# A decoder step on one core: lent token places that hold raw weights longer

## The chip, the cores and the metric

The kernel is one program on one core of a Trainium2 chip. The time is the device time of one execution in microseconds (us); lower is better. Engines are named as the profile names them: PE is TensorE (PEld its weight loads), DVE is VectorE, ACT is ScalarE, POOL is GpSimd, SP is SyncE, whose queue issues most loads. SBUF is the on-chip memory, PSUM holds TensorE's sums.

## What is computed

One step of a hybrid decoder layer, on 2048 prompt tokens and 64 new tokens (8 sequences of 8) that attend to 8192 cached positions through a page table. All data are float32.

```
h  = rmsnorm(x, g1);  z = h @ w_in                     # 1024 -> 3072: B, C, U, Q, K, V
y_conv = B * conv3(C * U)                              # 512 channels, width 3
o  = softmax(q1 k1 + alibi) v - lam * softmax(q2 k2 + alibi) v   # 4 heads, causal
o  = rmsnorm(o, subln) * (1 - lam0)
x  = x + concat(y_conv, o) @ w_out                     # 1024 -> 1024
h2 = rmsnorm(x, g2)
x  = x + relu(h2 @ w_up)**2 @ w_down                   # 1024 -> 4096 -> 1024
y  = rmsnorm(x, final_g)
```

The outputs are y for prompt and new tokens, the keys, the values and the last two rows of C * U.

## The kernel before

**Products in three parts.** A float32 product is made of three: each operand is split into a high half in a reduced format and the rest as a low half, and TensorE adds high x high, high x low and low x high. A raw weight (`wraw`, 128 x 1024, 512 KB) is loaded through SP's queue, ScalarE makes its high half `wh` (L254), VectorE its low half `wl` (L256), and TensorE reads those two. There are four buffers for each of `wh` and `wl`, and two places of its own for raw weights.

**Stages.** First the input projection, then the prompt's attention, together with the last convolution and the first tokens' output projection. From about 1140 us on it is output projection and MLP: four blocks of 384 prompt tokens (blocks 0 to 3, three tiles of 128 rows) and then a last block with 512 prompt tokens and the 64 new ones. Beside blocks 0 to 3 runs decoding: attention of the new tokens to the cached pages. It is a generator whose small steps are emitted between TensorE's matmuls (`between`, `tick`), a fixed amount for so much matmul time. It gathers keys and values on GpSimd's queue (`kraw`, `vpg`, L727 and L735), transposes the keys on VectorE (`kt`, L745), and does small matmuls (L930, L965, L977).

**A block** (`Dense.run`). The MLP's 4096 columns are 32 units m in 16 chunks c of two units. `first_ups` makes four up units; then for c = 0 to 13 `down` takes the two units of chunk c (36 matmuls, x += ..., L1445), and `up` makes the two of chunk c + 2 (48 matmuls). The last two up units (c = 13) are made together in two halves, after each of which `before_last(g)` is called: it issues the loads of the next tokens' mixed activations (`load_mix`, four loads of 0.8 MB). Then come the down chunk 14, the output projection of the *next* block's tokens (`out_proj`), and the down chunk 15. Between chunks `poll` takes one entry of a list `rest`: the final norms and stores of the block before, loads of gains, and lending.

**The order of the weights** is written out by `mlp_weights`: u0 to u3; for c = 0 to 13 the two of down chunk c and the two of up chunk c + 2; down 14; eight of the output projection (four pairs of rows for each half of the 1024 columns); down 15: 72 in a block. `W.get()` takes the next, `W.ahead(n)` has the n after it split. When weight i is split, `back` frees its place and loads the raw weights as far as i + 2 (two places), or i + 5 while three places are lent. `out_proj` makes the first half of the columns for all three token tiles, weight by weight (72 matmuls), and adds to x after that (L1340); then the second half tile by tile (72 matmuls).

**Lending.** Token tiles lie in six places: `x1_0` and `x1_1`, three each, for even and odd blocks. Between the storing of one block's results and the loading of the block after the next, three are empty. `W.lend` makes them extra places for raw weights: in block 0 after c = 0, in blocks 1 to 3 at the twelfth entry of `rest`, that is at the end of c = 3. Before the change `take_back` ends this after c = 9: from then on the lent places are not refilled. After c = 11 `x_loads` puts the loads of the next tokens (`load_x`, L1274, 512 KB each) on `rest`, one for each poll. In block 3 the tokens of the last block are loaded in `before_last(0)`.

Emission is by hand (`manual_schedule`): each engine and queue takes its instructions in the order in which the program issues them, and waits for data and places by semaphores.

Of the kernel before, what the change touches and what calls it, by code (L numbers as in the profile page):

```python
# [62 lines left out]
NDS = 4  # L63
# [4 lines left out]
def tile_hymba_step(  # L68
# [124 lines left out]
    def drain():  # L193
        while dec["gen"] is not None:
            step()
# [8 lines left out]
    class Weights:  # L204
# [9 lines left out]
        def lend(self, slots):  # L214

            self.lent = list(slots)
            self.extra += slots
            self.load(len(self.srcs))

        def take_back(self):  # L220

            self.lent, self.extra = [], []

        def back(self, i):

            slot = self.held.pop(i, None)
            if slot is None:
                self.own += 1
            elif slot in self.lent:
                self.extra.append(slot)  # L230
            self.load(i + 1 + self.rb + len(self.lent))

        lent = []
# [107 lines left out]
    W = Weights(lo, [wview[:, :, c0:c0 + P] for o in orders for _, _, c0 in o], 2, 2)  # L341
# [797 lines left out]
    for j in range(1, 4 * H):  # L1139
        h, g = divmod(j, 4)  # L1140
        after = gidx[16 * ((j - 5) // 4) + 15] if j >= 5 else -1
        due.setdefault(max(gidx[4 * j] - 3, after, -1), []).append((load_k, h, g))
        after = gidx[16 * ((j - VB) // 4) + 15] + 3 if j >= VB else -1
        due.setdefault(max(gidx[4 * j], after), []).append((load_v, h, g))
    for j in range(1, 8 * H):
        after = gidx[2 * (j - 3) + 1] if j >= 3 else -1
# [41 lines left out]
    NC = NF // CH  # L1188
# [27 lines left out]
    class Dense:  # L1216
# [261 lines left out]
                                               op0=ALU.mult, op1=ALU.mult)  # L1478
                eng.dma_start(out=dst[r0:r0 + n, :], in_=y[:n])

        def run(self, ub, poll, before_last, nxt, after, x_loads=lambda: None):
            self.ub = ub
            self.first_ups()
            for c in range(NC - 2):
                self.down(range(c * CH, (c + 1) * CH))
                poll()
                if c == NC - 7:
                    W.take_back()
                if c == NC - 5:
                    x_loads()  # L1490
                ms = range((c + 2) * CH, (c + 3) * CH)
                if c < NC - 3:
                    for m in ms:
                        self.up(m)
                        poll()
# [598 lines left out]
    sb1 = c1.enter_context(tc.tile_pool(name="mlp_sb1", bufs=1, reuse_waits="tile"))  # L2094
# [3 lines left out]
    box = {}  # L2098
    rest = []
# [2 lines left out]

        rest.append(lambda: W.lend([(xb, f"x1_{(i + 1) % 2}{ti}") for ti in range(3)]))

    def x_loads():
        while rest:
            rest.pop(0)()
        assert not W.held
        nxt = ds[cur[0] + 1] if cur[0] < NDS - 1 else None
        if nxt:  # L2110
            rest.extend(lambda ti=ti: nxt.load_x(ti) for ti in range(3))

    lend(0)

# [15 lines left out]
    def poll():  # L2130
        switch()
        if rest:
            rest.pop(0)()
        elif box and box["todo"] and cur[0] == NDS - 1:
            box["todo"].pop(0)()

    def before_last(g):
        while rest:
            rest.pop(0)()
        if cur[0] < NDS - 1:  # L2140
            ds[cur[0] + 1].load_mix(0, [g])
            return
        drain()
        switch()
        while box["todo"]:
            box["todo"].pop(0)()
        if g == 0:
            for ti in range(3):
                box["d"].load_x(ti)

    cur = [0]
    for i, d in enumerate(ds):
        cur[0] = i
        d.run([(sb1, "uh", "ul", 4, 384)], poll, before_last, lambda: ds[cur[0] + 1] if cur[0] < NDS - 1 else box["d"], None, x_loads)
        rest += [lambda: load_gain("f", nc.gpsimd)] + FN * [lambda: None]
        for ti in range(4):
            rest += [lambda d=d, ti=ti: d.final(ti, nc.gpsimd), lambda: None]
        if i < NDS - 1:
            rest.append(lambda: load_gain("2", nc.gpsimd))
        if i < NDS - 1:  # L2160
            lend(i + 1)
# [40 lines left out]
```

## Time and profile before

| | us |
|---|---|
| three runs, median (lowest to highest) | 3179.14 (3163.96 to 3181.11) |
| the profiled execution, its own time | 3178.61 |
| its span from first to last instruction | 3176.7 |
| TensorE busy in it | 3024.5 |
| mean granted TensorE clock (1 is 2.4 GHz) | 0.982 |

The profile is of one execution. A line such as L254 is a line of the kernel; "out<-in" gives the tiles by the program's names. Busy time counts overlapping instructions once; what ended an idle time stands behind an arrow. A clock below 1.00 in a stretch means that TensorE was granted its lower level (1.2 GHz) for a part of it. The DMA share is the mean busy share of the core's 16 DMA engines. A matmul's own record is longer than its pace, since matmuls overlap.

### The profile page before, as it was taken

Reading aid. Unit: us, or ns where it says so; the run is one execution under the profiler, and the core shown is the slowest. Engines: PE = TensorE matmul, PEld = TensorE weight load, DVE = VectorE, ACT = ScalarE, POOL = GpSimd, SP = SyncE. Lnnn points to the kernel's source line nnn. Section 1 sums busy time; section 2 is a strip of 40 time slices with the busy share of each in tenths; the row PEclk is TensorE's granted clock in tenths of the full one; section 3 lists DMA queues with packets and bytes.
Section 4 is the critical chain, followed back from the end, with each engine's and each line's share of the span. In section 5 each row is a group of like instructions: output and inputs, shape, how many; then the busy total and the mean of one; then the engine's idle time right before and its main releaser. Section 6 shows DMA issues by size and latency. Waiting matters only on the chain.

```text
span 3176.7 us, 55329 instructions
## 1 busy us (share of the span) xinstructions
PE 3024.5 (95%) x21670; PEld 2590.5 (82%) x21670; DVE 1956.6 (62%) x4121; ACT 1334.2 (42%) x2873; POOL 779.9 (25%) x1002
## 2 busy tenths in 40 slices
PE   7998998999999999998999999999999999999998
PEld 7987888989997788876778767787677887888887
DVE  5466353277888667766676666776566554664445
ACT  3323323367778643342334324433334433333332
POOL 1012364311122120122434443444324430000000
PEclk9999999999999999999999999999999999999999
DMA  5766886744435356676788786887767756232222
GB/s 153 226 226 202 292 283 196 248 126 106 124 102 153 110 183 209 210 249 231 246 275 285 247 293 229 287 290 264 273 204 248 248 164 201 73 100 80 80 80 70
DMA packets 443294, 624.73 MB, mean 197 GB/s; under 512 B 36661, under 2 KB 337717, under 8 KB 426650
## 3 DMA queue, kind: packets, MB, share of 16 engines
q1 hardware_dynamic: 379594, 338.82, 34.4%
q0 software_dynamic: 62272, 278.96, 24.9%
q8 instruction: 171, 2.80, 0.4%
q10 hardware_dynamic: 1168, 3.41, 0.3%
q14 instruction: 89, 0.73, 0.1%
HBM read 565.35 MB, written 55.74 MB: 196 GB/s over the span
## 4 chain that ended last, share of the span: by engine, by line
PE 70%; DVE 10%; DMA 9%; issue 5%; ACT 3%; POOL 3%; SPq 0%; ACTq 0%; DVEq 0%; POOLq 0%
PE ups L200 7%; PE dps L1438 6%; PE ups L202 6%; PE ups L201 6%; PE dps L1439 6%; PE dps L1440 6%; PE ps L200 5%; PE ps L202 5%; PE ps L201 5%; PE asc L1864 4%; DMA wraw<-in_w_up_dram 3%; PE O L1951 3%; PE sps L930 3%; PE o_ps L977 3%; DVE kt L745 2%
## 5 line engine op out<-in xcount | busy, mean ns | idle before, releaser
L256 DVE TENSOR_TENSOR wl<-wraw,wh 128x1024 fp32r<-128x1024 f32 x408 | 497.7, 1220 | 330.4 <-ACT wh L254 324.7
L254 ACT CAST wh<-wraw 128x1024 fp32r<-128x1024 f32 x408 | 424.3, 1048 | 598.2 <-PE dps L1440 257.9
L735 POOL DMA_INDIRECT vpg<-in_cache_v_dram,pt x512 | 533.6, 1042 | 323.8 <-PE o_ps L977 178.6
L200 PE MATMUL ups<-h2h,wh 128*128 128x384 f32 (+2 forms) x1520 | 506.5, 333 | 14.2 <-DVE x L1445 8.1
L202 PE MATMUL ups<-h2h,wl 128*128 128x384 f32 (+2 forms) x1520 | 493.2, 324 | 3.9 <-DVE wl L256 3.9
L201 PE MATMUL ups<-h2l,wh 128*128 128x384 f32 (+2 forms) x1520 | 492.1, 324 | 0.0
L1438 PE MATMUL dps<-wh,uh 128*128 128x512 f32 (+1 forms) x1076 | 436.9, 406 | 7.3 <-ACT wh L254 4.7
L1439 PE MATMUL dps<-wl,uh 128*128 128x512 f32 (+1 forms) x1076 | 426.7, 397 | 14.9 <-DVE wl L256 14.2
L1445 DVE TENSOR_TENSOR x<-dps,x 128x512 f32<-128x512 f32 (+1 forms) x534 | 356.2, 681 | 114.8 <-PE dps L1440 114.1
L1440 PE MATMUL dps<-wh,ul 128*128 128x512 f32 (+1 forms) x1076 | 424.4, 394 | 0.0
L200 PE MATMUL ps<-hh,wh 128*128 128x384 f32 (+1 forms) x1152 | 404.9, 351 | 1.1 <-ACT cc L1558 0.7
L202 PE MATMUL ps<-hh,wl 128*128 128x384 f32 (+1 forms) x1152 | 377.7, 328 | 2.9 <-DVE wl L256 2.9
L201 PE MATMUL ps<-hl,wh 128*128 128x384 f32 (+1 forms) x1152 | 376.7, 327 | 0.1
L727 POOL DMA_INDIRECT kraw<-in_cache_k_dram,idxk x128 | 125.6, 982 | 938.9 <-DVE kt L745 922.4
L200 PEld LDWEIGHTS ups<-h2h,wh 128*128 128x128 f32 x1520 | 288.1, 190 | 49.2 <-issue 35.5
L1397 DVE TENSOR_TENSOR ul<-r,uh 128x384 fp32r<-128x384 f32 (+2 forms) x190 | 99.9, 526 | 370.4 <-ACT uh L1396 370.2
L745 DVE STREAM_TRANSPOSE kt<-kraw 128x512 f32<-128x512 f32 x512 | 317.7, 678 | 0.0
L202 PEld LDWEIGHTS ups<-h2h,wl 128*128 128x128 f32 x1520 | 288.0, 189 | 4.8 <-DVE wl L256 4.8
L201 PEld LDWEIGHTS ups<-h2l,wh 128*128 128x128 f32 x1520 | 288.4, 190 | 2.3
L1394 ACT ACTIVATE r<-ups 128x384 f32<-128x384 f32 (+2 forms) x190 | 88.2, 464 | 423.1 <-PE ups L202 423.1
L1438 PEld LDWEIGHTS dps<-wh,uh 128*128 128x128 f32 (+1 forms) x1076 | 200.2, 186 | 75.6 <-issue 23.8
L1439 PEld LDWEIGHTS dps<-wl,uh 128*128 128x128 f32 (+1 forms) x1076 | 200.6, 186 | 61.2 <-DVE wl L256 23.0
(273 smaller groups left out, 4764.3 us busy)
## 6 DMA issues: line engine op xcount, KB each, us to landing
wraw<-in_w_up_dram SPq DMA_DIRECT2D x160, 512.0 KB
wraw<-in_w_down_dram SPq DMA_DIRECT2D x160, 512.0 KB
wraw<-in_w_in_dram SPq DMA_DIRECT2D x72, 512.0 KB
wraw<-in_w_out_dram SPq DMA_DIRECT2D x40, 512.0 KB
x<-in_x_prompt_dram SPq DMA_DIRECT2D x27, 512.0 KB
vpg<-in_cache_v_dram,pt POOLq DMA_INDIRECT x512
qt<-QH SPq DMA_DIRECT2D x64, 128.0 KB
qt<-QL SPq DMA_DIRECT2D x64, 128.0 KB
```

The lines of the kernel that those rows point to most:

```text
L200: nc.tensor.matmul(ps, lhsT=wh, rhs=ah, start=first, stop=False)
L201: nc.tensor.matmul(ps, lhsT=wh, rhs=al, start=False, stop=False)
L202: nc.tensor.matmul(ps, lhsT=wl, rhs=ah, start=False, stop=last)
L254: nc.scalar.copy(wh, t)
L256: eng.tensor_sub(wl, t, wh.bitcast(F32))
L735: nc.gpsimd.indirect_dma_start(out=t[:, g, :], out_offset=None, in_=cv, in_offset=bass.IndirectOffsetOnAxis(ap=idxv[:, 4 * it + g:4 * it + ...
L745: nc.vector.transpose(t[:, e, 16 * j:16 * j + 16].rearrange("p a b -> p (a b)"), kraw[2 * r + e][:, 16 * j:16 * j + 16].rearrange("p a b - ...
L1438: nc.tensor.matmul(ps, lhsT=uh, rhs=wh[:, half], start=(i == 0), stop=False)
L1439: nc.tensor.matmul(ps, lhsT=uh, rhs=wl[:, half], start=False, stop=False)
L1440: nc.tensor.matmul(ps, lhsT=ul, rhs=wh[:, half], start=False, stop=(i == len(ms) - 1))
L1445: nc.vector.tensor_add(xx, ps, xx)
L1864: nc.tensor.matmul(ps[:, 0:N], lhsT=t[self.h, qg][:, c, qo:qo + P], rhs=kst[self.h, kc][:, c, 0:N], start=(k == 0), stop=(k == 1))
```

## The change

`take_back` moves from after c = 9 to `before_last`: behind the second half of the last up chunks in blocks 0 to 2, behind the first in block 3. It is given a function that loads a token tile into a place. Empty lent places get their tokens at once. A place that holds a raw weight gets them when that weight has been split: `back` then calls the function in place of returning the place. `x_loads` with its two calls in `run` is gone, and so are the three token loads of `before_last(0)` in block 3.

```diff
--- before.py
+++ after.py
@@ -217,9 +217,12 @@
             self.extra += slots
             self.load(len(self.srcs))
 
-        def take_back(self):
-
-            self.lent, self.extra = [], []
+        def take_back(self, freed):
+
+            self.freed = freed
+            empty, self.lent, self.extra = self.extra, [], []
+            for slot in empty:
+                freed(slot)
 
         def back(self, i):
 
@@ -228,6 +231,8 @@
                 self.own += 1
             elif slot in self.lent:
                 self.extra.append(slot)
+            else:
+                self.freed(slot)
             self.load(i + 1 + self.rb + len(self.lent))
 
         lent = []
@@ -1478,16 +1483,12 @@
                                                op0=ALU.mult, op1=ALU.mult)
                 eng.dma_start(out=dst[r0:r0 + n, :], in_=y[:n])
 
-        def run(self, ub, poll, before_last, nxt, after, x_loads=lambda: None):
+        def run(self, ub, poll, before_last, nxt, after):
             self.ub = ub
             self.first_ups()
             for c in range(NC - 2):
                 self.down(range(c * CH, (c + 1) * CH))
                 poll()
-                if c == NC - 7:
-                    W.take_back()
-                if c == NC - 5:
-                    x_loads()
                 ms = range((c + 2) * CH, (c + 3) * CH)
                 if c < NC - 3:
                     for m in ms:
@@ -2102,13 +2103,8 @@
 
         rest.append(lambda: W.lend([(xb, f"x1_{(i + 1) % 2}{ti}") for ti in range(3)]))
 
-    def x_loads():
-        while rest:
-            rest.pop(0)()
-        assert not W.held
-        nxt = ds[cur[0] + 1] if cur[0] < NDS - 1 else None
-        if nxt:
-            rest.extend(lambda ti=ti: nxt.load_x(ti) for ti in range(3))
+    def take_back(d):
+        W.take_back(lambda slot: d.load_x([t for _, t in d.xslots].index(slot[1])))
 
     lend(0)
 
@@ -2139,19 +2135,20 @@
             rest.pop(0)()
         if cur[0] < NDS - 1:
             ds[cur[0] + 1].load_mix(0, [g])
+            if g == 1:
+                take_back(ds[cur[0] + 1])
             return
         drain()
         switch()
         while box["todo"]:
             box["todo"].pop(0)()
         if g == 0:
-            for ti in range(3):
-                box["d"].load_x(ti)
+            take_back(box["d"])
 
     cur = [0]
     for i, d in enumerate(ds):
         cur[0] = i
-        d.run([(sb1, "uh", "ul", 4, 384)], poll, before_last, lambda: ds[cur[0] + 1] if cur[0] < NDS - 1 else box["d"], None, x_loads)
+        d.run([(sb1, "uh", "ul", 4, 384)], poll, before_last, lambda: ds[cur[0] + 1] if cur[0] < NDS - 1 else box["d"], None)
         rest += [lambda: load_gain("f", nc.gpsimd)] + FN * [lambda: None]
         for ti in range(4):
             rest += [lambda d=d, ti=ti: d.final(ti, nc.gpsimd), lambda: None]
```

## Rows read from the trace of the kernel before

**Rows 1.** The page's busy time by engine, and its group of ScalarE's high halves.

```profile
PE 3024.5 (95%) x21670; PEld 2590.5 (82%) x21670; DVE 1956.6 (62%) x4121; ACT 1334.2 (42%) x2873; POOL 779.9 (25%) x1002
...
L254 ACT CAST wh<-wraw 128x1024 fp32r<-128x1024 f32 x408 | 424.3, 1048 | 598.2 <-PE dps L1440 257.9
```

**Rows 2.** Waits of the whole span: who waited for whom, total, times, longest.

```profile
ACT wh L254 <- DMA wraw<-in_w_out_dram: 104.9, 27, 9.8
```

**Rows 3.** Windows: length, busy time by engine, clock, DMA share, GB/s.

```profile
2654.23:2662.44 8.21, 8.21 (x38) 6.71 (x37) 4.48 (x7) 2.48 (x4) 0.00 (x0) 1.00 1.03 328
1656.98:1678.82 21.84, 21.84 (x185) 17.70 (x184) 14.84 (x25) 8.61 (x17) 10.07 (x10) 1.00 0.82 289
1396.39:1422.12 25.73, 23.63 (x186) 18.90 (x185) 14.86 (x24) 8.80 (x16) 9.93 (x11) 0.93 0.86 274
1433.14:1457.11 23.97, 22.58 (x176) 15.86 (x174) 9.99 (x13) 6.78 (x11) 10.06 (x10) 1.00 0.96 348
1457.11:1483.53 26.42, 21.43 (x140) 16.25 (x137) 16.20 (x38) 7.00 (x10) 9.54 (x10) 0.87 0.64 227
1779.30:1803.56 24.26, 21.45 (x156) 17.97 (x155) 16.97 (x35) 8.06 (x13) 11.06 (x11) 0.93 0.73 249
1856.88:1884.50 27.62, 23.80 (x173) 17.19 (x172) 13.88 (x21) 6.75 (x11) 9.33 (x10) 0.94 0.80 273
1884.50:1907.82 23.32, 20.37 (x110) 14.35 (x109) 13.05 (x29) 7.04 (x14) 7.41 (x8) 1.00 0.66 234
2273.88:2295.54 21.66, 20.62 (x167) 14.72 (x166) 8.74 (x12) 5.92 (x11) 9.64 (x10) 1.00 1.00 374
2295.54:2325.12 29.58, 25.41 (x161) 17.87 (x160) 17.88 (x40) 7.92 (x11) 10.71 (x10) 0.88 0.59 217
2662.44:2723.64 61.20, 59.41 (x265) 44.38 (x264) 29.91 (x58) 16.15 (x22) 0.00 (x0) 1.00 0.20 69
```

**Rows 4.** Chain of waits behind block 0: start, length, what.

```profile
1419.95 15.26 DMA wraw<-in_w_out_dram
...
1437.62 7.42 DMA wraw<-in_w_out_dram
...
1447.45 7.07 DMA wraw<-in_w_out_dram
...
1462.38 1.77 DVE x L1340 x3
```

**Rows 5.** Chain of waits behind block 1.

```profile
1861.53 9.77 DMA wraw<-in_w_out_dram
...
1881.43 10.36 DMA wraw<-in_w_out_dram
```

**Rows 6.** VectorE's timeline at the projection behind block 2.

```profile
2294.25 1.23 DVE L256 TENSOR_TENSOR wl<-wraw,wh 128x1024 fp32r<-128x1024 f32 x1 [5.89 <-ACT wh L254]
...
2296.08 3.08 DVE L745 STREAM_TRANSPOSE kt<-kraw 128x512 f32<-128x512 f32 x5
...
2300.19 1.89 DVE L745 STREAM_TRANSPOSE kt<-kraw 128x512 f32<-128x512 f32 x3
2302.00 1.85 DVE L1340 TENSOR_TENSOR x<-ps,x 128x512 f32<-128x512 f32 x3
2303.77 1.21 DVE L256 TENSOR_TENSOR wl<-wraw,wh 128x1024 fp32r<-128x1024 f32 x1
```

**Rows 7.** VectorE's timeline in block 1, c = 11.

```profile
1783.49 1.23 DVE L256 TENSOR_TENSOR wl<-wraw,wh 128x1024 fp32r<-128x1024 f32 x1 [1.00 <-ACT wh L254]
```

**Rows 8.** SyncE's queue in block 0: the first and last of three token loads.

```profile
1365.36 0.98 SPq L1274 DMA_DIRECT2D x<-in_x_prompt_dram  x1
...
1387.77 0.43 SPq L1274 DMA_DIRECT2D x<-in_x_prompt_dram  x1
```

**Rows 9.** Chain of waits behind block 2 and in block 3.

```profile
2318.11 30.97 issue
...
2379.97 13.22 DMA wraw<-in_w_up_dram
```

## Prediction

> **What bounds the kernel now.** Begin with the engines: TensorE is busy 95% of the span [rows 1], so time can only be won where TensorE stands still or runs at its lower clock. The waits name the candidate for this change: ScalarE, which makes the high half of each weight (L254, 1.05 us [rows 1]), waited 27 times, 104.9 us in all, for the output projection's weights to land [rows 2]. That is ScalarE's idle time, not the kernel's. What of it reaches TensorE is read from stretches of equal work [rows 3]. Call T the start of a block's output projection (for the next tokens), 1433.14, 1856.88 and 2273.88 us for the projections behind blocks 0, 1 and 2. Number a block's weights as the list has them: 56 and 57 are the down weights of c = 13, 58 and 59 the last up weights, 60 and 61 the down weights of c = 14, 62 to 69 the projection's, 70 and 71 the last down weights.
>
> In the lent part of a block one pair of chunks takes 21.84 us with TensorE full and clock 1.00 (block 1, c = 5). The same work takes 25.73 us at c = 13 of block 0, and 24.26 at c = 11 of block 1, both behind the present take-back. The projection's first half takes 23.97, 27.62 and 21.66 us in the three blocks, its second half 26.42, 23.32 and 29.58, though a half is the same 72 matmuls with some decoding between. DMA is at 0.80 to 1.00 in the first halves and 0.59 to 0.66 in the second [rows 3].
>
> The chain of waits shows why. Behind block 0 it runs from one projection weight's landing to the next: 15.26, 7.42 and 7.07 us, then through VectorE's three additions at 1462.38 [rows 4]. Behind block 1 it is 9.77 and 10.36 us of the same [rows 5]. With two places, the load of weight i+2 cannot begin before weight i is split, so each landing sets the next. VectorE takes its instructions in order, and makes the trouble larger: behind block 2 the low half at 2294.25 waited 5.89 us, and behind it stood eight transposes for decoding (4.97 us), three additions (1.85) and then the low half that TensorE was waiting for, at 2303.77, 8 us after the second half had begun at 2295.54 [rows 3, 6].
>
> **The change part by part.** *What stays.* No matmul, split or byte is added. Three places take a token tile each and are loaded as often as before. So the sum is of waits alone.
>
> *Take-back at the last up chunks in place of c = 9.* After c = 9 the lead of raw weights no longer falls from five to two. Block 0, c = 13: 25.73 - 21.84 = 3.9 us gained. Block 1, c = 11: 2.4 us between the same two kinds of stretch, but VectorE idled only 1.00 us for the weight's high half [rows 7], and what follows there is decoding's step from one sequence to the next; I take 1.0, with bounds 0 and 2.4. The stall that I see in block 2's c = 11 and 12 belongs to that step too: 0.
>
> *The first half of the projection.* At the new take-back weights 62 to 66 lie raw in the five places. Of the eight, five are on chip before T, where now 64 is loading. I take block 2's first half as that of unhurried weights: it has the same decoding (167 TensorE instructions against 176 and 173) and clock 1.00. Gain 23.97 - 21.66 = 2.3 and 27.62 - 21.66 = 6.0, together 8.3 us.
>
> *The second half.* Its bare length: 36 matmuls take 8.21 us where nothing interferes [rows 3], so 72 take 16.4. Block 2's first half is 5.3 us above that for 95 instructions of decoding, 0.055 each. The second halves have 68, 38 and 89 more than 72, so they should take 20.2, 18.5 and 21.3 us; they are 6.2, 4.8 and 8.3 above it, 19.3 together, the low clock (0.87, 1.00, 0.88) included. Not all of it goes. Weights 68 and 69 need buffers that come free late, and their low halves are queued on VectorE behind the three additions: 1.85 + 2 x 1.23 us, against the 12 matmuls (2.7 us) that TensorE can do with 66 and 67: 1.5 us stays. Weight 69 goes out when 67 is split, about T + 18, and TensorE wants it 18 matmuls (4.1 us) into the second half, at T + 26; with the landings of 7 to 10 us above and 2.3 us of splitting it is 1 to 4 us late, on top of nothing that the 1.5 covers: another 1.5, the nearer end, since DMA is down to about 0.6 by then. With 3 us left in each of three blocks the gain is 19.3 - 9 = 10.3; bounds 0 (the gap stays) and 14.8 (only the first 1.5 stays).
>
> *The token loads, moved.* Now they go out early, in block 0 the first at 1365.36 and the last of the three at 1387.77, 75 us before the additions want them [rows 4, 8]. After the change each goes out on SP right behind the split of a lent weight. In which order follows from the lending, and when from the half's four quarters of 5.4 us (21.66 / 4): 64 is split at its start, 65, 66 and 67 with the second, third and fourth quarter, each split taking 1.05 + 1.23 us. In blocks 1 and 2 the two own places hold 22 and 23 when three more are lent, and places are refilled in turn, so 62 and 63 are own and 64, 65, 66 lent: tokens go out at about T + 2, T + 5 and T + 11. In block 0 lending comes at weights 8 and 9, so lent are 62, 65 and 66: about T - 9 (ahead of c = 14's down chunk, half of a 21.84 us pair), T + 5 and T + 11. They are wanted when the first half ends, T + 21.7 or later. From T + 11 there are 10.7 us; two of the three landings in rows 4 and both in rows 5 fit. On SP nothing but weights stands behind a token's load, and the one directly behind (67 or 68) waits for the same split or an earlier one, so SP adds no wait. But an own place stays empty from the split of 63 to that of 65, since loading then stops two weights ahead: the lead of five is spent once, in the projection, and not renewed. If a token is late, the addition blocks VectorE, and the low halves of 68 and 69 and then TensorE wait behind it. I take 1 us in each of three blocks, 3 in all; bounds 0 and 4.6 each (a landing of 15.26, as in rows 4).
>
> The Trainium skill speaks against this move: "DMA: Bandwidth & Descriptors", under Rules for kernel authors, says to issue a DMA early and wait for it late, so that its fixed cost is covered. By that rule the token loads should stay where they are; what it would cost here is the third rival below. The rows show the same rule broken today for the weights, whose landings are the chain.
>
> *Block 3.* Decoding has ended and DMA is at 0.20 in the projection behind it, from 2662.44 on [rows 3]; I count 0. The last block never lends.
>
> The sum: 3.9 + 1.0 + 8.3 + 10.3 - 3 = 20.5 us. The profiled execution took 3178.61 us (span 3176.7 and 1.9 outside it), the median of the three runs is 3179.14, so it stands for them. 3178.6 - 20.5 = 3158; with the small stalls that I have not named shifting a little either way, 3159. By its own bounds the likeliest case lies between 3178.6 - (3.9 + 2.4 + 8.3 + 14.8) = 3149 (no token late, only 1.5 us left in each second half) and 3163 (5.4 us won in the second halves in place of 10.3).
>
> A difference of 0.5% (16 us) is about what a measurement of this kernel can tell from none: its three runs span 17 us.
>
> **The rivals.** *The gap of the second half stays.* The same 1.5 MB that were tokens early are now in the projection, where DMA is at 1.00 and 374 GB/s in block 2's first half [rows 3]: 4 us of that bandwidth. If 67 to 69 are late by as much as they now are, only 3.9 + 1.0 + 8.3 - 3 = 10 us are won: 3168. For it: the DMA share. Against it: total bytes from take-back to the end of the projection are equal, three tokens for three weights, and tokens are wanted last.
>
> *Decoding and the short lead of the next block take it back.* Behind block 2 the chain runs over GpSimd's gathers, with a 30.97 us stretch that shows no reason, and then over a landing of 13.22 us in block 3's first chunks, where there are only two places before and after the change [rows 9]. If gathers and those landings set the pace, what is saved behind block 2 (8.3 - 3 - 1 = 4 us) and behind block 1 (6.0 + 4.8 - 3 - 1 = 7 us) is waited for again: a gain of 20.5 - 11 = 9 us, 3169. Against it: the row names no cause, and by the code a gather of keys is issued when VectorE has transposed the keys before it, which comes earlier too.
>
> *Tokens late: slower.* The three last landings before an addition decide. From a landing of 10.7 us on, each further us is a us of TensorE in each of three blocks. The gains above must be used up first: at 10.7 + 20/3 = 17.4 us the time is as before, at 23 us it is 3195. The longest landing in these rows is 15.26 us, in the midst of 3 MB of loads for the activations. That is what the rule of the Trainium skill named above would make of the change.
>
> *The change does not do what it says* (the lead is already lost before T, as when SP is held up by the activations' loads, which stay in front): 3176 to 3179.
>
> **How the numbers follow.** Chances: forecast 0.55, second half unchanged 0.22, taken back 0.13, tokens late 0.06, no effect 0.04. The time given is the forecast's. Eight in ten: from 3144 (the forecast's lower bound and the spread of runs) to 3180, which takes in the second, third and last cases; above lies the slow one. Faster by over 0.5% (under 3163) holds nearly all of the first case: 0.54. Within 0.5%: the rest of it, the second, third and last, and part of late tokens: 0.40. Slower: 0.06.
>
> **What would show it.** In block 0, c = 13 at about 22 us. First halves at 21 to 23 us in all three blocks and second halves at 21 to 25, clock near 1.00. ScalarE's wait for projection weights well under half of 104.9 us, the high halves of 64, 65 and 66 without a wait for DMA. Token loads between T - 9 and T + 12, and no VectorE addition (L1340) waiting for a DMA. Wrong would be: L1340 waiting for tokens, second halves still at 26 to 29 us, or the saving gone again in the first four pairs of chunks of the next block.

## The result, and the profile after

The changed kernel took 3143.86 us (median of five runs, 3142.37 to 3156.06); the kernel before, run beside it, 3173.44 (five runs, 3163.96 to 3181.11). The ratio is 0.9919, with a 95% interval of 0.9901 to 0.9936. The forecast's sum, 3158.1 of 3178.6, is a ratio of 0.9936: the direction was right, and the size stands at the small end of what was measured. In absolute terms the median is 15 us under the 3159 that was forecast, at the low end of its range (3144); 6 of these are the kernel before, which ran that much under its earlier median. The profiled execution took 3151.0 us, its span is 3149.0, 27.7 us shorter than before's. A profile is one execution, and these two ran over the medians of their kernels, by 5 us before and by 7 us after. Later lines of the code have moved by five (L254 is now L259, L256 is L261, L745 is L750, L1340 is L1345, the token loads are L1279).

The page and the waits of the whole span, in place of [rows 1] and [rows 2]:

```profile
PE 3011.3 (96%) x21670; PEld 2584.2 (82%) x21670; DVE 1956.1 (62%) x4121; ACT 1330.6 (42%) x2873; POOL 780.2 (25%) x1002
...
L259 ACT CAST wh<-wraw 128x1024 fp32r<-128x1024 f32 x408 | 422.6, 1048 | 506.9 <-PE dps L1445 298.7
```

```profile
ACT wh L259 <- DMA wraw<-in_w_up_dram: 67.9, 20, 11.1
...
ACT wh L259 <- DMA wraw<-in_w_out_dram: 38.1, 9, 14.9
```

ScalarE's wait for the projection's weights is down from 104.9 us to 38.1, from 27 waits to 9; but one wait of 14.9 is longer than any before. No row of the waits has L1345 waiting for a DMA: the tokens were never late.

The windows, in place of [rows 3], in this order: block 0's c = 13 and the two halves of the projection behind it; block 1's c = 11 and its two halves; block 2's two halves, then its c = 12, and its c = 13 with the down chunk 14.

```profile
1398.63:1420.48 21.85, 21.85 (x186) 17.65 (x186) 14.86 (x24) 8.48 (x16) 9.98 (x10) 1.00 0.91 300
1431.50:1454.31 22.81, 21.98 (x175) 15.92 (x173) 8.44 (x12) 4.92 (x7) 9.46 (x10) 1.00 1.02 378
1454.31:1482.20 27.89, 22.01 (x140) 16.45 (x138) 17.35 (x39) 7.57 (x14) 9.55 (x10) 0.88 0.62 212
1777.48:1798.90 21.42, 19.90 (x155) 17.06 (x155) 16.41 (x34) 7.89 (x13) 9.50 (x10) 1.00 0.77 260
1852.22:1873.94 21.72, 21.72 (x173) 16.00 (x172) 10.31 (x17) 5.15 (x10) 11.09 (x12) 1.00 1.04 389
1873.94:1896.59 22.65, 20.06 (x110) 14.32 (x108) 14.81 (x32) 7.03 (x14) 6.44 (x6) 1.00 0.58 197
2257.75:2281.07 23.32, 22.05 (x174) 15.95 (x173) 11.76 (x19) 5.14 (x10) 10.52 (x10) 1.00 1.03 394
2281.07:2302.71 21.64, 20.58 (x154) 15.19 (x152) 13.80 (x31) 6.51 (x8) 10.61 (x9) 1.00 0.67 248
2204.38:2223.79 19.41, 19.41 (x162) 16.54 (x161) 10.88 (x28) 7.26 (x17) 7.64 (x8) 1.00 0.78 272
2223.79:2257.75 33.96, 33.25 (x258) 25.40 (x257) 24.86 (x42) 15.60 (x31) 10.70 (x11) 1.00 0.67 239
```

Where TensorE's busy time equals the length, it was never idle. One row of before, 2273.88:2295.54 in [rows 3], does not hold a whole first half: at 2295.54 only 66 of its 72 matmuls had started. The whole one is

```profile
2273.88:2297.02 23.14, 22.10 (x174) 15.94 (x172) 10.22 (x17) 7.34 (x13) 9.64 (x10) 1.00 0.95 354
```

so behind block 2 the first half took 23.1 us, not 21.7, with 1.0 us of idle time, and the second half 28.1, not 29.6. Put against before, stretch by stretch (each from its first matmul to the first of the next stretch; the forecast's terms are added up by stretch):

| us | before | after | gain | forecast |
|---|---|---|---|---|
| block 0, c = 12 | 24.58 | 26.09 | -1.5 | 0 |
| block 0, c = 13 and down 14 | 36.75 | 32.87 | 3.9 | 3.9 |
| block 1, c = 10 and 11 | 46.10 | 43.26 | 2.8 | 1.0 |
| block 2, c = 12, 13 and down 14 | 60.96 | 53.37 | 7.6 | 0 |
| projection behind block 0 | 50.39 | 50.70 | -0.3 | 4.5 |
| projection behind block 1 | 50.94 | 44.37 | 6.6 | 6.8 |
| projection behind block 2 | 51.24 | 44.96 | 6.3 | 4.3 |
| all else | | | 2.3 | 0 |

So two things are to be explained: block 2's 7.6 us, which the forecast put at nothing, and block 0's projection, where it expected 4.5 and got none. Block 0's c = 12 stays open: it takes 24.6 us before and 24.6 to 27.4 in the other kernels of this document, however they lend.

**Block 0's projection.** T is 1431.50. SyncE's queue (start, time until the last of the group was issued), then the chain of waits:

```profile
1420.97 7.58 SPq L130 DMA_DIRECT2D mxh<-ATH  x2
1428.61 3.85 SPq L130 DMA_DIRECT2D mxl<-ATL  x2
1432.55 6.38 SPq L1279 DMA_DIRECT2D x<-in_x_prompt_dram  x2
1438.98 0.43 SPq L130 DMA_DIRECT2D wraw<-in_w_out_dram  x1
1439.72 0.33 SPq L1279 DMA_DIRECT2D x<-in_x_prompt_dram  x1
```

```profile
1436.29 2.27 DVE wl L261 x2
1438.58 0.35 SPq L1279
1438.98 13.89 DMA wraw<-in_w_out_dram
1452.98 1.06 ACT wh L259
...
1460.75 1.77 DVE x L1345 x3
1462.52 1.14 DVE wl L261
1463.70 0.80 PE ps L1333
1464.49 0.43 PE ps L1334
...
1469.58 0.23 PE ps L1332
```

Read it from the top. The activations' loads hold the queue from 1420.97 to 1432.46. The first two tokens come out behind them, the second only when VectorE has split the weight in its place (1438.56), and weight 67 stands behind that token: issued at 1438.98, it lands 13.89 us later. Between 1452.98 and 1460.75 lie the decoding's transposes (L750), then the three additions, then the low half that TensorE wants at 1463.70: the same order as in [rows 6], in another block. The price is seen in the window: 27.89 us, of which TensorE was idle for 5.88; and behind the idle time its matmuls go on at 0.43 us each until about 1469, then at 0.23, the granted clock of the half being 0.88.

**Block 2, c = 12 and 13.** All idle times of TensorE from c = 12 to the down chunk 14 before, then ScalarE and VectorE before, then VectorE after:

```profile
2215.70 0.50 PE L1439 MATMUL dps<-wl,uh 128*128 128x512 f32 x1 [1.70 <-DVE wl L256]
...
2229.45 0.41 PE L1011 MATMUL ops<-osum,osc 128*128 128x32 f32 x2 [2.08 <-DVE osc L1008]
...
2240.10 0.49 PE L1438 MATMUL dps<-wh,uh 128*128 128x512 f32 x1 [1.62 <-ACT wh L254]
...
2241.36 0.50 PE L1439 MATMUL dps<-wl,uh 128*128 128x512 f32 x1 [0.77 <-DVE wl L256]
```

```profile
2202.11 1.05 ACT L254 CAST wh<-wraw 128x1024 fp32r<-128x1024 f32 x1 [8.35 <-DMA wraw<-in_w_up_dram]
...
2226.24 1.05 ACT L254 CAST wh<-wraw 128x1024 fp32r<-128x1024 f32 x1 [5.23 <-DMA wraw<-in_w_up_dram]
```

```profile
2203.20 1.23 DVE L256 TENSOR_TENSOR wl<-wraw,wh 128x1024 fp32r<-128x1024 f32 x1 [3.34 <-ACT wh L254]
...
2205.62 3.08 DVE L745 STREAM_TRANSPOSE kt<-kraw 128x512 f32<-128x512 f32 x5
...
2227.32 1.23 DVE L256 TENSOR_TENSOR wl<-wraw,wh 128x1024 fp32r<-128x1024 f32 x1 [4.60 <-ACT wh L254]
2228.46 0.68 DVE L1445 TENSOR_TENSOR x<-dps,x 128x512 f32<-128x512 f32 x1
2229.06 0.34 DVE L1008 TENSOR_SCALAR osc<-o_ps,wr 128x128 f32<-128x128 f32 x1
```

```profile
2191.22 2.13 DVE L261 TENSOR_TENSOR wl<-wraw,wh 128x1024 fp32r<-128x1024 f32 x1
...
2194.57 3.08 DVE L750 STREAM_TRANSPOSE kt<-kraw 128x512 f32<-128x512 f32 x5
...
2212.13 1.26 DVE L261 TENSOR_TENSOR wl<-wraw,wh 128x1024 fp32r<-128x1024 f32 x1
2213.31 0.68 DVE L1450 TENSOR_TENSOR x<-dps,x 128x512 f32<-128x512 f32 x1
2213.95 0.35 DVE L1013 TENSOR_SCALAR osc<-o_ps,wr 128x128 f32<-128x128 f32 x1
```

The decoding's step from one sequence to the next (L745 to L1008) is the same in both. Before, two up weights came late, the low halves waited 3.34 and 4.60 us, and the step stood behind them on VectorE. So of the 6.2 us that TensorE idled, 2.1 ended with the step (L1008) and 4.1 with a high or low half of a weight. After, neither low half waits, and TensorE idles for 0.7 us.

### The profile page after: what moved, and what is told of

It is laid out like the page before. It is cut to its first block, busy times and chain, and to the rows that moved or that the text cites. A ratio compares the mean times of both kernels' runs of the same rounds, so it can differ in the third digit from the quotient of the medians.

```text
span 3149.0 us, 55349 instructions
## 1 busy us (share of the span) xinstructions
PE 3011.3 (96%) x21670; PEld 2584.2 (82%) x21670; DVE 1956.1 (62%) x4121; ACT 1330.6 (42%) x2873; POOL 780.2 (25%) x1002
## 4 chain that ended last, share of the span: by engine, by line
PE 74%; DVE 10%; DMA 8%; ACT 3%; issue 3%; POOL 1%; SPq 0%; ACTq 0%; DVEq 0%; POOLq 0%
PE ups L200 7%; PE dps L1443 7%; PE ups L202 7%; PE ups L201 7%; PE dps L1444 7%; PE dps L1445 7%; PE ps L200 5%; PE ps L202 5%; PE ps L201 4%; PE asc L1865 4%; PE O L1952 3%; PE sps L935 3%; PE o_ps L982 3%; DMA wraw<-in_w_up_dram 2%; DVE wl L261 2%
## 5 line engine op out<-in xcount | busy, mean ns | idle before, releaser
L261 DVE TENSOR_TENSOR wl<-wraw,wh 128x1024 fp32r<-128x1024 f32 x408 | 498.1, 1223 | 261.6 <-ACT wh L259 260.4
L259 ACT CAST wh<-wraw 128x1024 fp32r<-128x1024 f32 x408 | 422.6, 1048 | 506.9 <-PE dps L1445 298.7
L750 DVE STREAM_TRANSPOSE kt<-kraw 128x512 f32<-128x512 f32 x512 | 317.6, 677 | 0.0
L1443 PEld LDWEIGHTS dps<-wh,uh 128*128 128x128 f32 (+1 forms) x1076 | 200.3, 186 | 74.2 <-issue 23.4
```

What stands on the lines that cost most here:

```text
L259: nc.scalar.copy(wh, t)
L261: eng.tensor_sub(wl, t, wh.bitcast(F32))
L750: nc.vector.transpose(t[:, e, 16 * j:16 * j + 16].rearrange("p a b -> p (a b)"), kraw[2 * r + e][:, 16 * j:16 * j + 16].rearrange("p a b - ...
L1443: nc.tensor.matmul(ps, lhsT=uh, rhs=wh[:, half], start=(i == 0), stop=False)
```

## The experiments

Kernels of one group ran on one chip, and each ratio is to the kernel before on that chip: 3172.65 us in the first group, 3172.39 in the second, 3172.03 in the third, 3203.69 in the last. A group's stage sums are over blocks 0 to 2: c = 10 to down 14, first and second halves of the projection (before 301.6, 74.8, 77.8; changed kernel 288.8, 67.9, 72.2), and c = 0 to 3 of blocks 1 to 3 (287.8; 285.4). Each sum is of one profiled execution. The expectations call the theories by names. LEAD: the gain is the raw weights held ahead, until the projection takes them. CONTENTION: it is which transfers run beside each other. PROJECTION, and later ORDER, ask about the projection's own weights and tokens, and in which order they leave.

**One half of the change at a time.**

*The tokens late, the places empty from c = 10 on* (edit to the kernel before):

```diff
-        nxt = ds[cur[0] + 1] if cur[0] < NDS - 1 else None
-        if nxt:
-            rest.extend(lambda ti=ti: nxt.load_x(ti) for ti in range(3))
...
             ds[cur[0] + 1].load_mix(0, [g])
+            if g == 1:
+                for ti in range(3):
+                    ds[cur[0] + 1].load_x(ti)
```

> The kernel before (take-back after c = 9), with one edit: the three token loads of blocks 0 to 2 are not issued during c = 11 and 12 but together in before_last(1), so the lent places lie empty in between. Theory LEAD (the change wins because raw weights stay five ahead through c = 13 and into the projection): nothing is won, c = 11 to 13 of blocks 0 to 2 keep their stalls (within 3 us of before in sum) and the projections keep about 153 us in sum or get longer; 3170 to 3185 us. Rival CONTENTION (the change wins because 1.5 MB of token loads no longer run beside the weights of c = 11 to 13): the 13 us that the changed kernel won in c = 10 to 13 appear here too; about 3160 us.

Measured: 1.0026 (1.0005 to 1.0048), 3183.17 us; the profiled execution took 3173.77. The stages c = 10 to 14 fell to 292.1, by 9.5 us, of which 6.9 are block 2's c = 12 and 13, where the tokens ran before: CONTENTION holds there. Block 0's did not fall (97.5 for 97.4). The 2.8 of block 1's c = 11 (24.3 to 21.4) cannot be the tokens, since in the kernel before the first of them leaves at 1797.78, behind the stall; with the same early take-back it takes 24.3 and 25.6 in two runs below. The first halves took more back, 101.6 in place of 74.8; those behind blocks 0 and 1:

```profile
1431.60:1467.98 36.38, 24.54 (x175) 16.75 (x174) 14.13 (x22) 6.77 (x11) 9.54 (x10) 0.86 0.83 306
...
1856.74:1887.89 31.15, 23.88 (x173) 17.15 (x172) 13.78 (x21) 6.76 (x11) 9.10 (x10) 0.89 0.81 288
```

Moving the tokens alone makes the kernel no faster: they go out ahead of weights of which only two are on chip.

*The take-back earlier* (edits to the changed kernel: `early` calls `take_back` for the next block after c = 12, or, in a second kernel, after c = 9 as before the change; tokens still one by one):

```diff
                 poll()
+                if c == 12:
+                    early()
...
             ds[cur[0] + 1].load_mix(0, [g])
-            if g == 1:
-                take_back(ds[cur[0] + 1])
```

> The changed kernel with its take-back in blocks 0 to 2 moved from before_last(1) to the poll after the down chunk of c = 12, so that the lent places drain during c = 12 and 13 and the projection has two raw weights ahead as before. LEAD: c = 10 to 12 are won (some 8 to 13 us in blocks 0 to 2 together), the projections stay near the 153 us in sum of before; 3160 to 3168 us. Rival PROJECTION (nearly all the gain is the lead that the projection starts with): c = 10 to 13 give nothing by themselves; 3170 to 3175 us. Rival CONTENTION: token loads now run in c = 12 and 13, so stalls come back there and little is won.

> The changed kernel with its take-back in blocks 0 to 2 moved to the poll after the down chunk of c = 9, where it was before: only the other part of the change is left, that a place takes its token tile as soon as its weight is split (in c = 10) and not at polls from c = 11 on. LEAD: no change, 3168 to 3180 us, stage times of c = 11 to 13 and of the projections as before within a few us. Rival CONTENTION: tokens are on chip before c = 11, so c = 11 to 13 are free of them and win up to 13 us; 3160 to 3163 us.

Measured: 0.9971 (0.9951 to 0.9991) after c = 12, 0.9980 (0.9958 to 1.0002) after c = 9, both in the range that LEAD gave. After c = 12 the stages c = 10 to 14 keep nearly all of their gain (290.5), and the projection loses all of its own (76.8 and 78.6). After c = 9 they keep 3.6 us (297.9): 4.9 in block 2, less 1.3 lost in block 1. So the projection's gain hangs on the places being full when it begins, and block 0's c = 13 on their being full then: it takes 21.85 us in every kernel of the first three groups that takes the places back after c = 12 or later, and 23.5 to 25.9 with the take-back after c = 9. Block 2's gain comes from full places as well, but most of it also comes without them, if no token loads beside the weights.

*The places empty from c = 9 and lent again behind c = 13:*

```diff
+                if c == 9:
+                    parked = []
+                    W.take_back(parked.append)
+                if c == 13:
+                    W.lend(parked)
```

> The changed kernel, but the three places stand empty from c = 9 to c = 13: after c = 9 a place whose weight is split is parked, and after the down chunk of c = 13 the three are lent again, so that weights 62 to 66 lie raw when before_last takes them back. No lead in c = 10 to 13, the full lead in the projection, no token loads before the projection. LEAD in both places: the projections win the 12 us of the changed kernel (blocks 1 and 2 about 6 each, block 0 nothing), c = 11 to 13 keep stalls of before; 3158 to 3165 us. Rival CONTENTION: c = 11 to 13 lose their stalls too, as no tokens load there; about 3146 us. Rival PROJECTION: the same 3146 us, with the stages of c = 11 to 13 unchanged and more won in the projections.

Measured: 0.9987 (0.9966 to 1.0008), 3172.35 us: a miss. Five places at T are not enough. The three weights had to land just when DMA is busiest: the first halves rose to 80.7, and the down chunks 14 took 6.5 us more. The second halves fell to 62.9. The stages c = 10 to 14 took 303.7, nothing won. Without the down chunks 14, block 0's and block 1's c = 10 to 13 kept their stalls (175.1 before, 177.3 here) with no token beside them, as LEAD had it, and block 2's fell by 6.6, as with the late tokens.

**What holds the projection.** All edits are to the changed kernel.

*Own places refill at once, with no limit of two ahead, when nothing is lent any more:*

```diff
-            self.load(i + 1 + self.rb + len(self.lent))
+            self.load(i + 1 + self.rb + len(self.lent) if self.lent else len(self.srcs))
```

> Against the changed kernel (0.992 of the kernel before): after the take-back an own place refills as soon as it is empty, and not only when the weights lead by fewer than the own places. LEAD: the last out weights (67 to 69) are issued before the tokens and the activations' loads that hold the queue in block 0, so block 0's second half falls from 27.9 us to 21 to 23, blocks 1 and 2 stay within 1 us of 22.7 and 21.6; the three second halves sum to 64 to 67 (72.2), the time is 0.989 to 0.991 of before. CONTENTION: the loads run earlier beside the stages c = 10 to 14 and lengthen those or the first halves by as much; all stages of c = 10 to the projection together stay within 3 us of 428.8, the time 0.991 to 0.994.

*Lending each place as soon as its tile's result has been sent, not all three behind the last:*

```diff
-            self.lent = list(slots)
+            self.lent = self.lent + list(slots)
...
-            rest += [lambda d=d, ti=ti: d.final(ti, nc.gpsimd), lambda: None]
+            rest.append(lambda d=d, ti=ti: d.final(ti, nc.gpsimd))
+            rest.append((lambda s=d.xslots[ti - 1]: W.lend([s])) if ti and i < NDS - 1 else lambda: None)
...
-            lend(i + 1)
```

> Each tile's place is lent right after its result has been sent, and not all three together behind the last of them: the three more weights are loaded some groups earlier in blocks 1 to 3. LEAD: the stages c = 0 to 3 of blocks 1 to 3 have some 29 us above the 85.4 that they would take at block 0's pace without the work beside them (16, 3 and 10); if late weights make these, 5 to 20 us of them go (285.4 falls to 265 to 280), and the time is 0.986 to 0.990 of before. CONTENTION: the stages c = 0 to 3 are held by what the results' stores and the loads move together, and no order of the loads helps: 283 to 290, the time 0.991 to 0.994.

*Lending two entries of `rest` later:*

```diff
+    rest += 2 * [lambda: None]
     lend(0)
...
+            rest += 2 * [lambda: None]
             lend(i + 1)
```

> The three places are lent two groups later, so that at the take-back they hold the out weights 62, 63 and 64 instead of 60 to 62 or so, and the places come empty, and the tokens go out, later or in another order against 65 to 69. PROJECTION: in the run whose places were re-lent the second halves summed to 62.9 us because the tokens did not run beside 67 to 69; if the places' contents at the take-back decide it, the second halves sum to 62 to 67 here (72.2), the first halves stay within 3 us of 67.9, and the time is 0.988 to 0.991 of before. Rival: what made those second halves short was the lead lost before them (their first halves were 13 us longer); then the sum of both halves stays at 137 to 144 (140.0) here, and the time is 0.991 to 0.994.

*No token loads:*

```diff
+        def zero(slot):
+            ti = [t for _, t in d.xslots].index(slot[1])
+            x = d.x1[ti] = slot[0].tile([P, D], F32, tag=slot[1], name=f"x1_{ti}")
+            nc.gpsimd.memset(x, 0.0)
+
-        W.take_back(lambda slot: d.load_x([t for _, t in d.xslots].index(slot[1])))
+        W.take_back(zero)
```

> The tokens of the three lent places of each block are not loaded (their places are filled with zeros by GpSimd, so x is left out of those tiles' sums); the weights keep their order. It shows what the tokens' loads cost the projection. CONTENTION: the 3 MB beside the last out weights are what holds those: block 0's second half falls from 27.9 to 21 to 23, the three second halves sum to 63 to 66 (72.2), first halves 64 to 68, the time 0.988 to 0.990 of before. LEAD: what holds weight 67 is that it is issued late, behind the activations' loads, and it is late without the tokens too: block 0's second half stays above 25.5, the time is 0.991 to 0.993.

(The tokens of a block are 1.5 MB; the expectation's 3 MB is a slip.) Measured:

| | ratio (95%) | c = 10 to 14 | first halves | second halves | second half, block 0 |
|---|---|---|---|---|---|
| changed kernel | 0.9919 (0.9901 to 0.9936) | 288.8 | 67.9 | 72.2 | 27.9 |
| refill at once | 0.9924 (0.9899 to 0.9948) | 288.7 | 67.7 | 67.4 | 23.3 |
| lend each | 0.9913 (0.9889 to 0.9937) | 288.6 | 68.4 | 71.0 | 26.9 |
| lend later | 0.9932 (0.9909 to 0.9955) | 291.2 | 69.8 | 70.9 | 28.7 |
| no tokens | 0.9904 (0.9883 to 0.9925) | 288.4 | 70.1 | 58.6 | 19.2 |

The run without tokens measures what they cost. The second half behind block 0 and both halves behind block 1, in its windows,

```profile
1452.38:1471.58 19.20, 19.20 (x140) 14.95 (x138) 10.72 (x26) 6.73 (x10) 8.71 (x10) 1.00 0.76 272
1841.75:1863.47 21.72, 21.72 (x173) 15.99 (x172) 12.35 (x19) 6.20 (x11) 13.93 (x15) 1.00 0.99 355
1863.47:1882.75 19.28, 19.28 (x109) 14.43 (x108) 12.99 (x29) 6.02 (x13) 6.41 (x6) 1.00 0.56 193
```

have no idle time at all and clock 1.00. So a second half costs some 19.2 us bare (20.1 behind block 2, with more decoding), and the second halves pay 72.2 - 58.6 = 13.6 us for the tokens in three blocks, 8.7 of them in block 0. The first half behind block 0 grew, though (24.8 at clock 0.93, from 22.8), so over both halves it is 11.4 us in three blocks and 6.7 in block 0. The time shows less: the ratio is lower by 0.0015, some 5 us, and the intervals overlap. LEAD's 25.5 for block 0's second half fell; CONTENTION's numbers for the halves were missed too (58.6 for 63 to 66, 70.1 for 64 to 68). And the run takes away two things at once, the tokens' bytes and their places in SyncE's queue: weight 67 leaves at 1429.02, T + 1.4, in place of T + 7.5. Refilling at once takes half of block 0's 8.7 from the second half, and then the tokens come last:

```profile
DVE x L1345 <- DMA x<-in_x_prompt_dram: 3.8, 3, 1.8
```

For this run LEAD's fall in block 0 nearly came (23.3 for 21 to 23), but not its time; CONTENTION's time came, but not its stages (some 424 us from c = 10 to the projection, for 426 to 432). Lending sooner leaves c = 0 to 3 as they are (285.2), as CONTENTION had it; 285.4 and 282.5 with the others show that these stages move by a few us from one profile to the next anyway. Lending later leaves the sum of both halves at 140.7 (140.0): this is what the rival expected, so the order of the places does not explain the run with the places lent again.

*Tokens by GpSimd's queue, or ahead of the activations' second half:*

```diff
-        W.take_back(lambda slot: d.load_x([t for _, t in d.xslots].index(slot[1])))
+        W.take_back(lambda slot: d.load_x([t for _, t in d.xslots].index(slot[1]), nc.gpsimd))
```

```diff
+            if g == 1:
+                take_back(ds[cur[0] + 1])
             ds[cur[0] + 1].load_mix(0, [g])
-            if g == 1:
-                take_back(ds[cur[0] + 1])
```

> The changed kernel with one edit: the tokens' loads of the take-back are issued by GpSimd and not by SyncE. In block 0 SyncE was held from 1421 to 1432.5 us by the loads of the mixed activations, the tokens stood behind these, and weight 67 behind the second token, which itself waited for its place. ORDER (the queue decides): the first tokens leave before 1428 us, weight 67 at 1433 to 1437 instead of 1439.0, block 0's second half falls from 27.9 us to 21 to 25, the three second halves sum to 64 to 69 (72.2; without tokens 58.6), the time is 0.988 to 0.991 of before. CONTENTION (the bytes decide, whichever queue they leave by): the second halves sum to 69 to 75, the time is 0.990 to 0.994. Rival: GpSimd waits for a place with the decoding's gathers behind it; then VectorE's kt stand before DMA waits in the projection, and the time is 0.993 to 0.998.

> The changed kernel with the take-back moved ahead of the loads of the second half of the mixed activations, on the same queue: the tokens whose places are empty by then go out ahead of these loads and of the 11.5 us for which block 0's queue is held by them. ORDER: as my prediction had it, one or two tokens of block 0 leave at 1412 to 1420 us, weight 67 at 1433 to 1437, block 0's second half is 21 to 25 us (27.9), the time 0.988 to 0.991 of before. Rival: in blocks 1 and 2 the activations of the second half land later for the tokens ahead of them, and the first halves grow by 2 to 5 us each (67.9 to 72 to 78); the time is 0.992 to 0.996. CONTENTION: all stages of c = 10 to the projection stay at 425 to 432 (428.8).

Measured: 0.9902 (0.9877 to 0.9926) by GpSimd, second halves 66.6, block 0's 23.4; 0.9921 (0.9898 to 0.9945) ahead of the activations, second halves 67.9, block 0's 27.9, and 428.9 for all stages from c = 10 to the projection, as CONTENTION had it. The second edit moved nothing in block 0: its first tokens still left at 1430.93 us, T + 1.0. No place is empty at the take-back, and the first that comes empty does so while the queue is held. GpSimd's queue shows the first token leaving early, as the forecast had assumed (T - 9); the other two leave later than it had them. SyncE's queue, GpSimd's tokens, the chain's row of weight 67, and a row of the waits, with T at 1428.79:

```profile
1418.87 8.26 SPq L130 DMA_DIRECT2D mxh<-ATH  x2
1427.18 3.75 SPq L130 DMA_DIRECT2D mxl<-ATL  x2
1431.04 19.79 SPq L130 DMA_DIRECT2D wraw<-in_w_out_dram  x3
```

```profile
1422.72 0.61 POOL L1279 DMA_DIRECT2D x<-in_x_prompt_dram  x1
...
1442.40 0.58 POOL L1279 DMA_DIRECT2D x<-in_x_prompt_dram  x1
...
1448.06 0.59 POOL L1279 DMA_DIRECT2D x<-in_x_prompt_dram  x1
```

```profile
1431.04 16.98 DMA wraw<-in_w_out_dram
```

```profile
DVE x L1345 <- DMA x<-in_x_prompt_dram: 3.9, 2, 3.7
```

The first token leaves at T - 6.1, weight 67 at T + 2.3 in place of T + 7.5. It lands at T + 19.2 in place of T + 21.4: of 5.2 us in the queue, 2.1 came out at the landing, since it now takes 16.98 us in place of 13.89. Both theories hold a part: of block 0's second half the order cost some 4.5 us (27.9 to 23.4), and the bytes the other 4.2 (to 19.2); over both halves it is 3.3 and 3.4 (50.7, 47.4, 44.0). These are differences between single profiles. The Trainium skill, in "DMA: Bandwidth & Descriptors", Rules for kernel authors, says that spreading loads over SP, ACT and GpSimd does not help the bandwidth and saves only time in the issuing sequencer. This trace agrees: in block 0's first half the DMA share is 1.02 with the one queue and 1.04 with the two, and what was won is a wait in SyncE's queue.

*Both edits together, and the changed kernel again:*

> Both edits that shortened block 0's second half: the own places refill at once after the take-back, and the tokens are issued by GpSimd. ORDER: weight 67 can leave neither earlier than its place is split nor faster than the tokens beside it let it, so the two gains do not add: the second halves sum to 63 to 67 (72.2 with neither, 67.4 and 66.6 with one), the time is 0.988 to 0.991 of before. If they add, the sum falls to 59 to 63, near the 58.6 without tokens, and the time to 0.987 to 0.989. Rival: the tokens come last in the sharing and the first adds of the projection wait for them by more than the 3.8 us that the refill alone showed; first halves above 72, time 0.991 to 0.994.

> The changed kernel once more, on the same chip as the last combination: 0.990 to 0.994 of before, and a second profile of it shows which stages repeat: c = 10 to 14 within 2 us of 288.8, block 0's second half 27 to 29 us, blocks 1 and 2 within 3 us of 22.7 and 21.6, the stages c = 0 to 3 of blocks 1 to 3 anywhere in 279 to 291.

Measured on this last chip: 0.9938 (0.9915 to 0.9961) together, 0.9930 (0.9910 to 0.9951) for the changed kernel. Together the edits gain nothing that shows, as the rival had the time, though not for its reason (first halves 66.7, not above 72); the second halves were 68.7 with both and 66.5 in the changed kernel. The ratio of the changed kernel repeats, but its stages do not, here: c = 10 to 14 took 301.6 in place of 288.8, block 0's second half 23.2 in place of 27.9, so two of the numbers expected were missed. Block 0 lost time one stage earlier here, in the down chunk 14 (15.7 us in place of 11.0), and that chunk and the projection together took 62.5 us, in place of 61.7 in the first profile of the changed kernel. With both edits they took 58.3 here; with one edit, on the other chips, 56.7 (refill) and 58.4 (GpSimd). In these single profiles the two gains do not add up. There is no profile of the kernel before on this chip, so what the stages gain over it here is not known. No kernel of this part can be told from the changed one: the intervals overlap.

## Why the prediction was right in sign, and where its sum was off

- **What bounds the kernel: right.** TensorE's busy share went from 95 to 96%, and the waits that the forecast named fell by two thirds.
- **Block 0, c = 13: right**, 25.73 to 21.85 us with 3.9 forecast. **Block 1, c = 11: sized low**: 24.26 to 21.42, 2.8 us, over the 2.4 that were the upper bound; 1.0 had been taken. The bound was no bound: c = 11 has 156 TensorE instructions, the stretch of 21.84 that it was measured from 185. The decoding's step was rightly seen there, and 1.5 us of idle time stay.
- **"The stall that I see in block 2's c = 11 and 12 belongs to that step too: 0" is the step that failed** (they are c = 12 and 13 as the change counts them), by 7.6 us. The decoding's step is on the chain, but ends only 2.1 of the 6.2 us of idle time, and it is a follower: it stood on VectorE behind low halves that waited for late weights. The runs bear it out: c = 12 of block 2 takes 19.4 us in all six kernels of the second and third group, which keep the late take-back, 22.1 with the take-back after c = 9, and 23.7 before; with empty places but no tokens loading beside them it takes 20.1 and 20.5. So it is the late weights, which five places or the tokens' absence make timely, and not the places as such.
- **First halves: right behind block 1** (27.62 to 21.72, 5.9 of 6.0), half of it behind block 0 (1.2 of 2.3). The match behind block 1 is luck: the 21.66 us of block 2 from which both gains were taken held 66 of the 72 matmuls. The whole half took 23.1 us, with 1.0 of idle time; taken from it the gains would have been 4.5 and 0.8. A first half without idle time takes 21.72 (block 1, after), near 21.66 by chance.
- **Second halves, block 0: failed.** The forecast had the first token at T - 9 and asked what stands behind a token's load on SyncE. It did not ask what stands ahead: the activations' loads, which stay in front, are in its last rival alone, at a chance of 0.04 and for the weights. They held the queue to T + 1, the tokens stood behind them, and weight 67 behind a token that waited for its place. The run by GpSimd's queue puts this part at 4.5 us of the second half (3.3 of both halves), and the run without tokens shows the rest: the tokens' bytes beside 67 to 69. The forecast had named second halves of 26 to 29 us as a sign of being wrong. Its bare lengths, 20.2, 18.5 and 21.3 us, were nearly right: the run without tokens has 19.2, 19.3 and 20.1. In blocks 1 and 2, where tokens left at T + 2 to T + 14 and T + 5 to T + 9, the projection won 12.9 us of 11.1 forecast.
- **Tokens late, -3: no such wait** in the changed kernel; in block 0 the weight was late instead. The 3.8 and 3.9 us of the runs that put weights first show that one of the two pays.
- **The rivals.** "The gap of the second half stays" came true in block 0 alone, for a reason next to the one given. "Taken back in the next block" did not: c = 0 to 3 of blocks 1 to 3 took 285.4 us in place of 287.8. The time of "Tokens late: slower" came in the first experiment, with the tokens moved and nothing lent in their place, at 1.0026, but not its mechanism: no row of its waits has L1340 waiting for a token; ScalarE waited 119.7 us for the projection's weights. There the Trainium skill's rule to issue early and wait late, which the forecast weighed, was broken for the weights; in the change it is kept for the weights at the tokens' cost, and the weights are the chain.
- **The total** was nearer than its parts: 9.4 us more than forecast in block 1's and block 2's c = 10 to 14, 1.5 less in block 0's, 3.0 less in the projection, and 2.3 elsewhere, which is within what stages move between profiles.

What stays open: why the last chip takes 1% longer with each kernel, and why the stalls of the changed kernel lie in other stages there; and how much of the differences of a few us between single profiles would repeat.

## What to carry to other kernels

In this kernel a buffer that waited empty for a tile wanted late was worth more as a place for the stream that is on the chain. Give it up one piece at a time, when the stream has drained it, and fill it while DMA has room (lending again in the busiest stretch gave 0.9987, keeping them to the change between blocks 0.9919). When a load is moved, list what stands ahead of it in its queue at the new time as well as what stands behind. A stall that follows an engine's own step is charged to that step only if what stood ahead of it in that engine's order was on time.

## What the runs showed of the hardware

A 512 KB load took 13.89 us from issue to landing, and 16.98 when it left 5.2 us sooner, in stretches where the 16 DMA engines show a share of 1.02 and 1.04 and move 378 and 382 GB/s: of the earlier issue only 2.1 us were left at the landing. After idle time of 5.48 us on TensorE, the 18.50 us behind it (1463.70 to 1482.20), without a gap, had a granted clock of 0.85 (matmuls at 0.43 us in place of 0.23 up to about 1469), so some 2.8 us more by estimate (18.50 x 0.15). The second half behind block 0 is 8.7 us longer than bare; 5.88 are idle time, and about 2.8 that clock.
